# Band attention in a two-layer encoder trunk: edge blocks, and every second pair's middle blocks, copied once as float32 instead of split in two

## Chip, cores, metric

One Trainium2 chip, one of its cores. The metric is the device time of one execution, in microseconds (us). All inputs and the output are float32.

## What is computed

Two layers over 1024 tokens of width 1024. Each layer has three groups of attention heads that read one input projection, and then a SwiGLU feed-forward part:

```python
proj = h @ w_in[l]
qa, ka, va, qb, kb, vb, qc, kc, vc = split_cols(proj, IN_SPLITS)
ya = neighborhood_attention(qa, ka, va, rpb_na[l])            # group A: 4 heads, 8 x 16 neighbours on a 16 x 64 grid
yb = sliding_window_attention(qb, kb, vb, sink_sw[l], t5_table) # group B: 6 heads, |i-j| <= 128, sink logit
yc = axial_attention(qc, kc, vc, gq_ax[l], gk_ax[l])           # group C: 6 heads, dense
y = jnp.concatenate([rms_norm(ya, ga), rms_norm(yb, gb), rms_norm(yc, gc)], axis=-1)
x = x + gt_a * (y @ w_o[l])
```

Inside a head: scores q k^T with a bias, softmax over the keys, then the product of the probabilities with v. Heads are 64 wide.

## The kernel before

**Numbers.** TensorE multiplies float32r operands in one pass each, and float32r keeps fewer bits than float32. Operands are therefore split into a rounded part ("hi") and a rest ("lo"). ScalarE (ACT) makes hi by a converting copy, VectorE (DVE) makes lo by a subtraction (`split_pt`, line 1258). The tile `vs` holds hi and lo of v side by side (64 columns each), so one product with `vs` as the stationary operand gives both parts of v, and `combine` (line 1294) adds the two halves: ACT copies one half out of PSUM, DVE adds the other. A product of probabilities with v thus takes two matmuls, one with the hi and one with the lo of the probabilities.

**Tiles.** Work comes in pairs: 256 queries of one head, as two blocks of 128. A head has four pairs, p = 0 to 3. Group C is dense (`PairC`, 24 pairs in a layer). Groups A and B are banded (`Band`, `PairA`, `PairB`: 16 + 24 = 40 pairs in a layer). For group A the tokens are reordered by columns of the grid, so that its window is a band too. A query block sees its own key block and one to each side. Over a pair there are two *middle* key blocks, seen by all 256 queries, and up to two *edge* blocks: the left one is seen by the first 128 queries only, the right one by the last 128. The pairs p = 0 and p = 3 have one edge block, p = 1 and 2 have two; that makes six in a head and 60 in a layer.

**One band pair**, step by step:

- `qk(c)`, c = 0, 1: two matmuls of 384 columns (256 where the sequence ends), one DVE instruction that adds bias and takes the row maximum (tiles `pr<-sA`, `pr<-sB`), one exponential on ACT with row sums.
- `divide`: a DVE reciprocal of the row sum (`rs<-rs`) and a scaling of the row on POOL (`scale_rows`), once for each c. It is put on the list `unfinished` and taken from there after the next `turn`.
- `turn(0)`: four TensorE transposes of the middle blocks into the PSUM tile `T`, then `split_pt` into two tiles `pt` (ACT then DVE).
- `turn(1)`: one or two transposes of the edge blocks, then `split_pt` into the tile `edge`, which is 256 columns wide for each edge block; the half of the queries that does not see the block is filled with zeros once, in `edges_make`.
- `pv(part)`: matmuls of `vs` with `pt` and `edge` into the PSUM tile `pv`, all 256 columns wide, two for each block. Two pairs share one `pv` tile (512 columns); there is one such tile (`psV`, one buffer), and after the odd pair `combine` empties it.

**Order.** One loop (line 1597) runs over the stream of the 64 pairs of a layer, C then A then B. Step n turns pair n, multiplies pair n-1, and makes the scores of pair n+3, or n+5 in the bands. The last pairs share TensorE with the first rows of the output projection (`ps_o`). In this stage only POOL's order is pinned to the text (line 1595); the orders on TensorE, ACT, DVE and the DMA queue are laid out by the tile framework when the program is built. A statistics step of an earlier group (`ps_st`: float32 sums over partitions by matmul; `isq`: DVE) falls into the stage too.

Every recorded operation has line 49 (the helper `issue`), so the profile is read by tiles.

Of the kernel before, what the change touches and what calls it, by code (L numbers as in the profile page):

```python
# [10 lines left out]
F32 = mybir.dt.float32  # L11
F32R = mybir.dt.float32r
# [7 lines left out]
P = 128  # L20
# [56 lines left out]
def f32(ap):  # L77
    return ap.bitcast(F32)
# [7 lines left out]
def trunk(ctx: ExitStack, tc, A, C, out):  # L86
    nc = tc.nc
    pe, act, dve, pool, sp = (
        Engine(tc, e) for e in (nc.tensor, nc.scalar, nc.vector, nc.gpsimd, nc.sync)
    )  # L90
# [28 lines left out]
    ident = idp.tile([P, P], F32, name="ident")  # L119
# [6 lines left out]
    ident, ones = f32(identr), f32(onesr[:, 0:1])  # L126
# [692 lines left out]
    for l in range(2):  # L819
# [308 lines left out]
        def scale_rows(pr, r):  # L1128
            pool.tensor_scalar(
                out=pr, in0=pr, scalar1=r, scalar2=1.0, op0=ALU.mult, op1=ALU.mult  # L1130
            )
# [14 lines left out]
                pr, s, AF.Exp, bias=rs[:, c : c + 1], accum_out=rs[:, 2 + c : 3 + c]  # L1146
            )

        def divide(pr, rs, c):
            dve.reciprocal(rs[:, 4 + c : 5 + c], rs[:, 2 + c : 3 + c])  # L1150
            scale_rows(pr, rs[:, 4 + c : 5 + c])

        first_pairs = []

        def early_scores():

            p = len(first_pairs)
# [11 lines left out]
            return lambda: [divide(prs[c], rs, c) for c in range(2)]  # L1169

        for oc in range(NE, 8):
            w = wab
# [48 lines left out]
        zB = [bz_tile() for _ in range(2)]  # L1221
        pad(atp, 16)
        gss = {23: gss_tile()}
        edge = []

        def edges_make():
            for _ in range(2):
                e = atp.tile([P, 2, 2, 256], F32R, name="edge", tag="edge", bufs=2)
                for z in range(2):
                    pool.memset(f32(e[:, z, 0, 128:256]), 0.0)  # L1230
                    pool.memset(f32(e[:, z, 1, 0:128]), 0.0)
                edge.append(e)

        edges_used = [0]

        def next_edge():
            edges_used[0] += 1
            return edge[edges_used[0] % 2]

        def edge_ap(e, z, left, right):  # L1240
            flat = e[:, z, :, :].rearrange("p e q -> p (e q)")
            if left and right:
                return flat.rearrange("p (a q) -> p a q", a=4)[:, 0:4:3, :]
            return flat[:, None, 0:128] if left else flat[:, None, 384:512]

        def pt_tile():
            return wp.tile([P, 4, 256], F32R, name="pt", tag="whl", bufs=8)

# [3 lines left out]
        def rs_tile():  # L1252
            return atp.tile([P, 8], F32, name="rs", tag="rs", bufs=6)
# [4 lines left out]
        def split_pt(T, hi, lo):  # L1258
            act.copy(hi, T)
            dve.tensor_tensor(out=lo, in0=T, in1=f32(hi), op=ALU.subtract)  # L1260

        class Pair:
# [5 lines left out]
            def __init__(self, row, vh, p):  # L1268
                self.row, self.vh, self.p = row, vh, p
                self.rs = rs_tile()  # L1270

            def finish(self, c, pr):

                unfinished.append(lambda: divide(pr, self.rs, c))

            def products(self, movs, part):
                if part == 0:
                    if self.p % 2 == 0:
                        open_pv[0] = psV.tile([P, H], F32, name="pv", tag="V")
                    self.pvt = open_pv[0]  # L1280
                cols = slice((self.p % 2) * 256, (self.p % 2) * 256 + 256)
# [45 lines left out]
        unfinished = []  # L1327

        class PairC(Pair):
# [5 lines left out]
            def qk(self, c):  # L1335
                pr = self.pr[c] = pr_tile()
                c_scores(self.h, 2 * self.p + c, c, pr, self.rs)
                self.finish(c, pr)

            def turn(self, c):  # L1340
                if c == 0:
# [9 lines left out]
            def pv(self, part):  # L1351
                self.products(
                    [
                        (kb * 4 + i, self.pt[kb][0][:, i, :], self.pt[kb][1][:, i, :])
                        for kb in range(2)
                        for i in range(4)
                    ],
                    part,
                )
# [38 lines left out]
        class Band(Pair):  # L1398
# [10 lines left out]
            def qk(self, c):  # L1409
                rs, p, sk = self.rs, self.p, self.sk  # L1410
                if c == 0:
                    self.s = psS.tile([P, 2, 512], F32, name=self.name, tag="S")
                s, pr = self.s, self.pr
                j = 2 * p + c
                a, b = self.spans[c]
                for i in range(2):
                    pe.matmul(
                        s[:, c, a:b], self.q[:, j * P : (j + 1) * P],
                        self.k[i][:, (j - 1) * P + a : (j - 1) * P + b],
                        start=(i == 0), stop=(i == 1),  # L1420
                    )
# [12 lines left out]
                self.finish(c, pr[:, c, a:b])  # L1434

            def turn(self, c):
                pr = self.pr
                T = t_tile()
                if c == 0:
                    self.pt = [pt_tile() for _ in range(2)]  # L1440
                    for b in range(2):
                        for i in range(2):
                            pe.transpose(
                                T[:, 2 * b + i, :], pr[:, b, (1 - b + i) * P : (2 - b + i) * P],
                                ident,
                            )
                    hv, lv = (
                        t[:, 0:2, :].rearrange("p i (c q) -> p c i q", c=2) for t in self.pt
                    )
                    split_pt(T.rearrange("p (c i) q -> p c i q", c=2), hv, lv)  # L1450
                    return
                e = self.e = next_edge()
                ne = 0
                if self.left:
                    pe.transpose(T[:, ne, :], pr[:, 0, 0:P], ident)
                    ne += 1
                if self.right:
                    pe.transpose(T[:, ne, :], pr[:, 1, 2 * P : 3 * P], ident)
                    ne += 1
                split_pt(  # L1460
                    T[:, 0:ne, :],
                    edge_ap(e, 0, self.left, self.right),
                    edge_ap(e, 1, self.left, self.right),
                )
# [132 lines left out]
        for n in range(-AHEAD - 1, N + 1):  # L1597
# [22 lines left out]
                    (v_back if n else v_store)(j)  # L1620
            if n == 50:
                yq = qk_tile()
            if n == 8:
                edges_make()
            if n == 54:
                wst = [w_o_stage(k) for k in korder[:2]]
            if n in (55, 59):
# [735 lines left out]
```

## Time and profile before

| | us |
|---|---|
| Median of 3 runs | 2432.55 (2431.05 to 2435.31) |
| The profiled execution, its own time | 2435.83 |
| Its span (first to last instruction) | 2434.1 |
| TensorE (PE) busy | 2362.9 |
| DVE busy | 1785.1 |
| ACT busy | 1203.9 |
| POOL busy | 759.6 |

How to read it: the durations of matmuls overlap, because TensorE is pipelined, and a 256-column matmul is shown with about 0.28 us although the next may start much earlier. A busy PE is therefore not a PE at its peak; what one matmul takes of the engine is read from the distance of the starts in a run of them. "PEld" is the loading of stationary operands beside that. DVE and ACT durations overlap a little too. The stage of the bands lies once in each layer: from the last `combine` of group C to the last of group B, that is 393.2 to 505.8 us in the first layer and 1580.0 to 1692.4 us in the second.

### The profile page before, as it was taken

How to read it: one execution, taken by the hardware profiler on the slowest of the kernel's cores; microseconds unless marked ns; L12 is line 12 of the kernel's file. 1: busy time of each engine (PE TensorE's matmuls, PEld its weight loads, DVE VectorE, ACT ScalarE, POOL GpSimd, SP SyncE). 2: the span in 40 equal slices, each digit the busy share in tenths (PEclk: the TensorE clock that was granted, in tenths of full speed). 3: DMA queues.
4: the chain of work that ended last, by engine and by line, in shares of the span. 5: the costliest groups of instructions: out<-in, count | busy, mean ns of one | idle time of the engine just before them, and what ended most of it. 6: DMA issues, size and time to landing. Idle time of an engine off the chain costs nothing.

```text
span 2434.1 us, 33735 instructions
## 1 busy us (share of the span) xinstructions
PE 2362.9 (97%) x11733; PEld 1963.3 (81%) x11733; DVE 1785.1 (73%) x2950; ACT 1203.9 (49%) x2290; POOL 759.6 (31%) x741
## 2 busy tenths in 40 slices
PE   8999999999999999999999999999999999999998
PEld 5778888788788788788787879987877888888886
DVE  5756899976967788586677589998787545547865
ACT  3421788954543333344543148887454333334443
POOL 1530344620244444300036114464004444430001
PEclk9999999999999999999999999999999999999999
DMA  8478215154245454596434861242534422329643
GB/s 262 151 237 269 61 27 148 43 181 148 87 143 178 156 183 150 166 276 195 144 96 113 277 187 27 58 125 68 191 96 136 142 100 96 103 101 305 206 129 108
DMA packets 305338, 356.98 MB, mean 147 GB/s; under 512 B 51964, under 2 KB 221788, under 8 KB 305168
## 3 DMA queue, kind: packets, MB, share of 16 engines
q1 hardware_dynamic: 283296, 342.07, 44.5%
q10 hardware_dynamic: 21504, 12.59, 2.0%
q8 instruction: 93, 1.52, 0.3%
q14 instruction: 77, 0.63, 0.1%
q0 software_dynamic: 368, 0.17, 0.0%
HBM read 269.79 MB, written 88.63 MB: 147 GB/s over the span
## 4 chain that ended last, share of the span: by engine, by line
PE 50%; DVE 4%; issue 4%; ACT 2%; POOL 1%; DMA 1%; ACTq 0%; SPq 0%; POOLq 0%; DVEq 0%
PE ps_w L49 21%; PE ps_d L49 14%; PE ps_o L49 3%; PE pv L49 2%; PE ps_ab L49 2%; PE ps_v L49 2%; PE T L49 2%; PE sC L49 2%; DMA qkd<-qko 1%; ACT pr L49 1%; PE ps_c L49 1%; POOL ct L49 1%; DVE pt L49 0%; PE ps_st L49 0%; DVE pr L49 0%
## 5 line engine op out<-in xcount | busy, mean ns | idle before, releaser
L49 PE MATMUL ps_d<-wpt 128*128 128x512 f32 x1848 | 424.3, 390 | 2.2 <-ACT wpt L49 1.9
L49 PEld LDWEIGHTS ps_d<-wpt 128*128 128x128 f32 x1848 | 345.6, 188 | 76.2 <-issue 3.0
L49 POOL TENSOR_SCALAR pr<-pr,rs 128x1024 f32<-128x1024 f32 (+2 forms) x248 | 192.8, 780 | 228.8 <-DVE rs L49 203.2
L49 POOL TENSOR_TENSOR sg<-sg,u 128x512 f32<-128x512 f32 x86 | 125.8, 1465 | 356.5 <-ACT sg L49 117.9
L49 PE MATMUL pv<-pt,vs 128*128 128x256 f32 x1088 | 182.5, 296 | 10.8 <-DVE y L49 3.6
L49 ACT CAST wpt<-w 128x512 fp32r<-128x512 f32 x154 | 95.7, 621 | 179.9 <-PE ps_d L49 161.4
L49 DVE TENSOR_TENSOR pt<-T,pt 128x512 fp32r<-128x512 f32 x272 | 178.2, 681 | 6.9 <-ACT pt L49 5.1
L49 PE MATMUL T<-identr,pr 128*128 128x128 f32 x1176 | 172.8, 273 | 1.0 <-DVE pt L49 0.5
L49 ACT CAST pt<-T 128x512 fp32r<-128x512 f32 x272 | 153.0, 586 | 37.8 <-PE T L49 35.8
L49 ACT COPY u<-ps_w 128x512 f32<-128x512 f32 x128 | 75.1, 587 | 193.1 <-PE ps_w L49 192.9
L49 POOL TENSOR_TENSOR wpt<-ws,wpt 128x512 fp32r<-128x512 f32 x80 | 112.3, 1405 | 179.0 <-ACT wpt L49 132.5
L49 DVE TENSOR_TENSOR wpt<-w,wpt 128x512 fp32r<-128x512 f32 x154 | 108.9, 707 | 80.6 <-ACT wpt L49 78.4
L49 PEld LDWEIGHTS pv<-pt,vs 128*128 128x128 f32 x1088 | 145.3, 189 | 27.6 <-DVE y L49 9.8
L49 PEld LDWEIGHTS T<-identr,pr 128*128 128x128 f32 x1176 | 138.2, 140 | 18.3 <-POOL pr L49 1.3
L49 DVE SCALAR_TENSOR_TENSOR acc<-wmt,condT,acc 128x512 f32<-128x512 f32 (+1 forms) x98 | 116.9, 1201 | 44.2 <-DMA wmt<-in_w_mod_dram 43.7
L49 ACT CAST wpt<-ws 128x512 fp32r<-128x512 f32 x176 | 107.7, 622 | 63.4 <-issue 28.2
L49 DVE TENSOR_TENSOR wpt<-ws,wpt 128x512 fp32r<-128x512 f32 x96 | 82.3, 868 | 62.9 <-ACT wpt L49 62.8
L49 DVE TENSOR_TENSOR wpt<-graw,wpt 128x512 fp32r<-128x512 f32 x154 | 109.2, 709 | 19.3 <-ACT wpt L49 19.3
L49 ACT CAST wpt<-graw 128x512 fp32r<-128x512 f32 x154 | 95.0, 617 | 48.2 <-DMA graw<-gpd 40.3
L49 DVE TENSOR_TENSOR ws<-wr 128x512 f32<-128x512 f32 x88 | 80.0, 911 | 49.2 <-POOL wpt L49 46.0
L49 PE MATMUL ps_w<-h22h,wpt 128*128 128x512 f32 x352 | 111.6, 399 | 4.3 <-ACT sg L49 3.6
L49 DVE TENSOR_REDUCE rs<-sC 128x1 f32<-128x1024 f32 x88 | 107.1, 1218 | 7.1 <-PE sC L49 5.2
(299 smaller groups left out, 6024.5 us busy)
## 6 DMA issues: line engine op xcount, KB each, us to landing
wr<-in_w_gu_dram SPq DMA_DIRECT2D x92, 512.0 KB, 4.1
gpd<-sg SPq DMA_DIRECT2D x154, 256.0 KB, 4.4
graw<-gpd SPq DMA_DIRECT2D x76, 512.0 KB, 3.5
w<-in_w_down_dram SPq DMA_DIRECT2D x110, 256.0 KB, 5.4
wmt<-in_w_mod_dram SPq DMA_DIRECT2D x48, 512.0 KB, 6.1
qk<-qkd SPq DMA_DIRECT2D x44, 512.0 KB, 6.7
wst<-in_w_o_dram SPq DMA_DIRECT2D x32, 512.0 KB, 3.9
wmt<-in_w_mod_dram SPq DMA_DIRECT2D x64, 256.0 KB, 3.8
```

Of the source, the lines that this page charges most:

```text
L49: ins = op(*args, **kwargs)
```

## The change

1. Edge blocks (all band pairs): the transposes in `T` are copied once, by DVE, into a float32 tile of one 128-column block each (three buffers), without a hi and lo; no ACT step, no zeros. `pv` multiplies each edge block once, float32 by float32, and only for the 128 queries that see it.
2. Middle blocks of odd pairs (p = 1 and 3): ACT copies `T` once as float32 into one tile `pt`; no subtraction on DVE. `pv` multiplies each of the two blocks once, float32 by float32, 256 columns. Even pairs keep the split in two.
3. All pairs, C too: the two rows' `divide` become one entry in `unfinished`, put there when the second row's scores are done: one reciprocal over two columns, then two scalings on POOL.

```diff
-        def divide(pr, rs, c):
-            dve.reciprocal(rs[:, 4 + c : 5 + c], rs[:, 2 + c : 3 + c])
-            scale_rows(pr, rs[:, 4 + c : 5 + c])
+        def divide(prs, rs):
+            dve.reciprocal(rs[:, 4:6], rs[:, 2:4])
+            for c, pr in enumerate(prs):
+                scale_rows(pr, rs[:, 4 + c : 5 + c])
...
-        def edges_make():
-            for _ in range(2):
-                e = atp.tile([P, 2, 2, 256], F32R, name="edge", tag="edge", bufs=2)
-                for z in range(2):
-                    pool.memset(f32(e[:, z, 0, 128:256]), 0.0)
-                    pool.memset(f32(e[:, z, 1, 0:128]), 0.0)
...
-            def finish(self, c, pr):
-                unfinished.append(lambda: divide(pr, self.rs, c))
+                self.parts = []
+            def finish(self, pr):
+                self.parts.append(pr)
+                if len(self.parts) == 2:
+                    unfinished.append(lambda: divide(self.parts, self.rs))
...
-                for n, (kc, a, b) in enumerate(movs):
+                for n, (kc, at, mvs) in enumerate(movs):
                     if (n < half) != (part == 0):
                         continue
-                    for i, mv in enumerate((a, b)):
+                    for i, mv in enumerate(mvs):
+                        v = vs[:, kc, self.vh, :]
                         pe.matmul(
-                            self.pvt[:, cols], vs[:, kc, self.vh, :], mv,
-                            start=(n == 0 and i == 0), stop=(n == len(movs) - 1 and i == 1),
+                            self.pvt[:, c0 + at.start : c0 + at.stop],
+                            v if mv.dtype == F32R else f32(v), mv,
+                            start=(n == 0 and i == 0),
+                            stop=(n == len(movs) - 1 and i == len(mvs) - 1),
+                            skip_group_check=True,
                         )
...
             def turn(self, c):
                 pr = self.pr
                 T = t_tile()
                 if c == 0:
-                    self.pt = [pt_tile() for _ in range(2)]
+                    whole = self.p % 2
+                    self.pt = [pt_tile() for _ in range(2 - whole)]
+                    if whole:
+                        self.pt = [f32(self.pt[0])]
...
+                    if whole:
+                        act.copy(to[0], T)
+                    else:
+                        split_pt(T, *to)
                     return
-                e = self.e = next_edge()
...
-                split_pt(
-                    T[:, 0:ne, :],
-                    edge_ap(e, 0, self.left, self.right),
-                    edge_ap(e, 1, self.left, self.right),
-                )
+                e = self.e = atp.tile([P, 2, P], F32, name="edge", tag="edge", bufs=3)
...
+                dve.tensor_copy(e[:, 0:n], T[:, 0:n])
 
             def pv(self, part):
                 k0, e = 2 * self.p, self.e
-                movs = [(k0 + i, self.pt[0][:, i, :], self.pt[1][:, i, :]) for i in range(2)]
+                movs = [
+                    (k0 + i, slice(0, 2 * P), [t[:, i, :] for t in self.pt]) for i in range(2)
+                ]
                 if self.left:
-                    movs.append((k0 - 1, e[:, 0, 0, :], e[:, 1, 0, :]))
+                    movs.append((k0 - 1, slice(0, P), [e[:, 0]]))
                 if self.right:
-                    movs.append((k0 + 2, e[:, 0, 1, :], e[:, 1, 1, :]))
+                    movs.append((k0 + 2, slice(P, 2 * P), [e[:, int(self.left)]]))
                 self.products(movs, part)
```

More of the change, by code (lines that the diff above doesn't have):

```diff
@@ L1168, in early_scores @@
             first_pairs.append(prs)
-            return lambda: [divide(prs[c], rs, c) for c in range(2)]
+            return lambda: divide(prs, rs)
         for oc in range(NE, 8):
@@ L1223, in trunk @@
         gss = {23: gss_tile()}
-        edge = []
-        def edges_make():
-            for _ in range(2):
-                e = atp.tile([P, 2, 2, 256], F32R, name="edge", tag="edge", bufs=2)
-                for z in range(2):
-                    pool.memset(f32(e[:, z, 0, 128:256]), 0.0)
-                    pool.memset(f32(e[:, z, 1, 0:128]), 0.0)
[L1232 to L1244, printed above, removed]
         def pt_tile():
@@ L1337, in qk @@
                 c_scores(self.h, 2 * self.p + c, c, pr, self.rs)
-                self.finish(c, pr)
+                self.finish(pr)
             def turn(self, c):
@@ L1353, in pv @@
                     [
-                        (kb * 4 + i, self.pt[kb][0][:, i, :], self.pt[kb][1][:, i, :])
+                        (kb * 4 + i, slice(0, 256), [t[:, i, :] for t in self.pt[kb]])
                         for kb in range(2)
@@ L1433, in qk @@
                 )
-                self.finish(c, pr[:, c, a:b])
+                self.finish(pr[:, c, a:b])
             def turn(self, c):
@@ L1446, in turn @@
                             )
-                    hv, lv = (
-                        t[:, 0:2, :].rearrange("p i (c q) -> p c i q", c=2) for t in self.pt
-                    )
-                    split_pt(T.rearrange("p (c i) q -> p c i q", c=2), hv, lv)
-                    return
-                e = self.e = next_edge()
[L1453 to L1459, printed above, removed]
-                split_pt(
-                    T[:, 0:ne, :],
-                    edge_ap(e, 0, self.left, self.right),
-                    edge_ap(e, 1, self.left, self.right),
-                )
+                    to = [t[:, 0:2, :].rearrange("p i (c q) -> p c i q", c=2) for t in self.pt]
+                    T = T.rearrange("p (c i) q -> p c i q", c=2)
+                    if whole:
+                        act.copy(to[0], T)
+                    else:
+                        split_pt(T, *to)
+                    return
+                e = self.e = atp.tile([P, 2, P], F32, name="edge", tag="edge", bufs=3)
+                n = 0
+                for left, here in ((True, self.left), (False, self.right)):
+                    if here:
+                        src = pr[:, 0, 0:P] if left else pr[:, 1, 2 * P : 3 * P]
+                        pe.transpose(T[:, n, :], src, ident)
+                        n += 1
+                dve.tensor_copy(e[:, 0:n], T[:, 0:n])
             def pv(self, part):
                 k0, e = 2 * self.p, self.e
-                movs = [(k0 + i, self.pt[0][:, i, :], self.pt[1][:, i, :]) for i in range(2)]
+                movs = [
+                    (k0 + i, slice(0, 2 * P), [t[:, i, :] for t in self.pt]) for i in range(2)
+                ]
                 if self.left:
-                    movs.append((k0 - 1, e[:, 0, 0, :], e[:, 1, 0, :]))
+                    movs.append((k0 - 1, slice(0, P), [e[:, 0]]))
                 if self.right:
-                    movs.append((k0 + 2, e[:, 0, 1, :], e[:, 1, 1, :]))
+                    movs.append((k0 + 2, slice(P, 2 * P), [e[:, int(self.left)]]))
                 self.products(movs, part)
@@ L1622, in trunk @@
                 yq = qk_tile()
-            if n == 8:
-                edges_make()
             if n == 54:
```

2 lines of the change are left out of this document (1 added, 1 removed).

## Prediction

> **What bounds the kernel now.** The change touches the band stage, once in each layer, so I read only that stage, and beside it the stage of group C, which runs the same loop. First the view of windows, which gives each engine's busy time in a stretch: the C stage, then the band stage of layer 0 and of layer 1.
>
> ```profile
> core 0: us, PE busy (x) PEld busy (x) DVE busy (x) ACT busy (x) POOL busy (x), PEclk, DMA share, GB/s
> 284.00:375.00 91.00, 90.58 (x650) 82.04 (x648) 85.50 (x138) 78.47 (x143) 40.43 (x43) 1.00 0.07 19
> 393.00:506.00 113.00, 105.41 (x714) 90.52 (x713) 103.21 (x339) 98.91 (x263) 65.31 (x111) 1.00 0.32 94
> 1580.00:1693.00 113.00, 105.63 (x714) 90.55 (x713) 103.43 (x339) 98.67 (x262) 65.39 (x111) 1.00 0.33 95
> ```
>
> The two band stages are alike to 0.3 us, so I work one out and double it. DVE is busy 103 of 113 us and ACT 99. PE's 105 holds overlapping durations, so I count its work. Its groups in the first band stage:
>
> ```profile
> L49 PE MATMUL T<-identr,pr 128*128 128x128 f32 x212 | 35.0, 274 | 0.5 <-DVE pt L49 0.3
> L49 PE MATMUL pv<-pt,vs 128*128 128x256 f32 x160 | 32.2, 302 | 3.5 <-DVE y L49 1.1 <-DVE rs L49 1.1 <-DVE pt L49 0.5
> L49 PE MATMUL pv<-edge,vs 128*128 128x256 f32 x120 | 22.6, 295 | 0.6 <-DVE edge L49 0.6
> L49 PE MATMUL sB<-qk 128*128 128x384 f32 x72 | 20.1, 365 | 0.0
> L49 PE MATMUL sA<-qk 128*128 128x384 f32 x32 | 8.7, 363 | 0.4 <-DVE rs L49 0.4
> L49 PE MATMUL ps_o<-qk,whi 128*128 128x512 f32 x24 | 8.2, 401 | 0.0
> L49 PE MATMUL sB<-qk 128*128 128x256 f32 x24 | 5.9, 326 | 1.3 <-DVE rs L49 1.1
> L49 PE MATMUL ps_o<-qk,wlo 128*128 128x512 f32 x12 | 4.9, 409 | 0.7 <-DVE wlo L49 0.7
> L49 PE MATMUL ps_st<-onesr,gss 128*128 128x1 f32 x32 | 3.7, 245 | 0.0
> L49 PE MATMUL sA<-qk 128*128 128x256 f32 x10 | 2.2, 316 | 0.0
> L49 PE MATMUL ps_r<-identr,rstd 128*128 128x128 f32 x16 | 2.1, 275 | 0.6 <-DVE rs L49 0.6
> ```
>
> What one takes of PE is the distance of starts. In the timeline (start, length of the run, count) it is the length less one instruction's own, over the count less one:
>
> ```profile
> 299.83 1.09 PE L49 MATMUL sC<-qk 128*128 128x512 f32 x4
> 300.75 1.03 PE L49 MATMUL T<-identr,pr 128*128 128x128 f32 x8
> ...
> 403.52 1.84 PE L49 MATMUL ps_st<-onesr,gss 128*128 128x1 f32 x16
> ...
> 423.37 0.64 PE L49 MATMUL pv<-edge,vs 128*128 128x256 f32 x4
> 423.85 0.28 PE L49 MATMUL pv<-pt,vs 128*128 128x256 f32 x1
> ```
>
> So 512 columns take (1.09 - 0.40) / 3 = 0.23 us, a transpose (1.03 - 0.27) / 7 = 0.109, `ps_st` (1.84 - 0.245) / 15 = 0.106, and 256 columns (0.64 - 0.28) / 3 = 0.12; 384 columns, three quarters of 0.23, take 0.175. The counts above times these: transposes 23.1 + 1.7, products 19.2 + 14.4, scores 18.2 + 4.1, `ps_o` 8.3, `ps_st` 3.4: 92.4 us of work. PE is idle 20.6 us of 113, DVE about 10, ACT about 14: no engine is full, three are nearly so. The same count in the C stage, from its three large groups:
>
> ```profile
> L49 PE MATMUL pv<-pt,vs 128*128 128x256 f32 x256 | 38.4, 292 | 0.3 <-DVE y L49 0.2
> L49 PE MATMUL sC<-qk 128*128 128x512 f32 x128 | 35.7, 399 | 0.2 <-ACT pr L49 0.2
> L49 PE MATMUL T<-identr,pr 128*128 128x128 f32 x264 | 35.3, 272 | 0.0
> ```
>
> 30.7 + 29.4 + 28.8 = 88.9 of 91 us: there PE is full, with DVE busy 85.5 beside it. What PE waits for in the band stage, from the view of waits over the same stretch (who waited for whom, total us, times, longest):
>
> ```profile
> PEld sB L49 <- DVE rs L49: 4.2, 13, 0.9
> PEld pv L49 <- DVE pt L49: 3.3, 9, 1.0
> ...
> PEld pv L49 <- DVE y L49: 2.6, 7, 0.7
> ```
>
> The first is a score tile not yet freed by DVE, the second the lo of the middle blocks, the third the one `pv` tile not yet emptied. All three end on DVE. So the band stage is set by DVE, closely followed by ACT, and PE has room.
>
> **The change, part by part** (for one layer: 40 pairs, 20 of them odd, 60 edge blocks).
>
> *PE, float32 products.* The trace has float32 products of 512 columns, with a one-column stationary operand:
>
> ```profile
> 31.95 1.02 PE L49 MATMUL ps_mod<-gm,condT 128*1 128x512 f32 x2
> 32.80 1.02 PE L49 MATMUL ps_mod<-ga,onesr 128*1 128x512 f32 x2
> ```
>
> Each call is two instructions, and the next call starts 0.85 us on. A call of 256 columns costs at least half, 0.425. At most each of its two instructions has also the 0.02 that 512 columns show above a quarter of 0.85 (0.23 against 0.2125), giving 0.465. I take 0.45, since the stationary operand here is 128 wide. An odd pair's two blocks went from 4 x 0.12 = 0.48 to 0.90 (0.85 to 0.93): +0.42, for 20 pairs +8.4 us (7.4 to 9.0). An edge block went from 2 x 0.12 = 0.24 to a call of 128 columns: at least 0.21 (a quarter of 0.85; also two of `ps_st`'s 0.106, which load a 128-wide float32 operand each), at most 0.25. I take 0.23: 60 times -0.01 is -0.6 (-1.8 to +0.6). PE's work rises by 7.8 (5.6 to 9.6), from 92.4 to 100.2.
>
> By the Trainium skill ("TensorE: Matmul & The Clock Gate", Back-to-back issue gap), a 128-column matmul in a stream with its weight loads takes about 81 ns; with the four passes that "FP8 and Floating Point Precision", TensorE Precision Notes, gives a true float32 product, an edge block would be estimated at 0.32 us and the sum below would come out about 11 us higher, at 2434. No row has a 128-column float32 product, and `ps_st`, nearest, points to the lower value.
>
> *DVE.* Its rows in the stage, a float32 copy out of PSUM from the start of the kernel, and a piece of its timeline:
>
> ```profile
> L49 DVE TENSOR_TENSOR pt<-T,pt 128x512 fp32r<-128x512 f32 x39 | 26.6, 682 | 0.7
> L49 DVE RECIPROCAL rs<-rs 128x1 f32<-128x1 f32 x70 | 11.0, 158 | 5.1 <-ACT pr L49 4.4
> ```
>
> ```profile
> L49 DVE COPY xt<-ps_x 128x512 f32<-128x512 f32 x4 | 2.5, 682 | 0.0
> ```
>
> ```profile
> 434.16 0.16 DVE L49 RECIPROCAL rs<-rs 128x1 f32<-128x1 f32 x1
> 434.24 0.28 DVE L49 TENSOR_TENSOR edge<-T,edge 128x128 fp32r<-128x128 f32 x1
> 434.42 0.69 DVE L49 TENSOR_TENSOR pt<-T,pt 128x512 fp32r<-128x512 f32 x1
> 435.02 0.16 DVE L49 RECIPROCAL rs<-rs 128x1 f32<-128x1 f32 x1
> ```
>
> The 20 subtractions of odd pairs go: at a distance of 0.60, -12.0 (-13.6 by duration). A copy out of PSUM takes 682 ns where the subtraction takes 682, so the edge steps stay at their price: 0. Half of the 70 reciprocals go, at 0.08: -2.8. DVE falls from 103.2 to 88.4.
>
> *ACT.* The edge casts go; the odd pairs' copy stays one instruction of 512 columns.
>
> ```profile
> L49 ACT CAST edge<-T 128x256 fp32r<-128x256 f32 x20 | 7.4, 370 | 1.0 <-PE T L49 0.7
> L49 ACT CAST edge<-T 128x128 fp32r<-128x128 f32 x19 | 5.0, 262 | 2.5 <-PE T L49 2.5
> ```
>
> That is -12.4 by duration, some -10.8 at DVE's ratio of distance to duration (0.60 to 0.69). ACT falls from 98.9 to about 88.
>
> *Costed at nothing.* The zeros on POOL go; POOL is busy 65 of 113. The joint reciprocal waits for the second exponential: the first row's scaling starts about half a step later, and POOL's next sink copies and norm work pass ahead of it; its result is due five pairs on (three in C), and a step is 113 / 40 = 2.8 us. On DVE, whatever stands behind that reciprocal (a bias addition or a copy of `T`) waits with it; the row above has 4.4 us of such waits for ACT now, over 70 instructions, so half of them gone bounds it at -2.2, and all of the old wait added once more at +4.4; I take 0. In the C stage DVE's saving lies beside a full PE: 0 (a reciprocal that came late there would show as PE idle above the 2.1 us of now).
>
> *The sum.* After the change PE has 100.2, DVE 88.4, ACT 88. Now the stage runs 113 - 103.2 = 9.8 us above its fullest engine, with three close together; the C stage runs 2.1 above its full PE. Afterwards PE leads by 12, which is like C, but the steps are as short and as chained as now (transpose, copy, product; product, `combine`, next product on the single `pv` tile), so I take a value nearer to today's: 8. The stage then takes 108.2, -4.8 a layer, -9.6 in all. The profiled execution of 2435.83 would take 2426.2; the median of the runs lies 3.3 below that execution, so it goes from 2432.55 to 2423.
>
> **Rivals.**
>
> *PE's idle time stays (slower).* If PE's 20.6 us of idle time are latencies of the chain and not DVE's queue, they stay, and PE's added work is paid in full: +7.8 a layer, +15.6 (11 to 19): 2448. The change is slower by more than 4.9 us in all once less than 5.4 of the 20.6 us go (7.8 - 2.4 a layer). For it: the `pv` tile has one buffer, and its wait (2.6 us) passes through both ACT and DVE. Against it: the two larger rows of the waits view end on DVE instructions that are removed or queue behind removed ones, and the C stage has the same single `pv` tile and hardly any idle PE.
>
> *The gain is eaten (no change).* Idle time falls by PE's added work and no more, to about 13 us: 2432, within 5 us. For it: three engines near 90% trade places, and the order on PE, ACT and DVE is laid out anew when the program is built. Against it: DVE and ACT each lose over 10 us.
>
> *Narrow float32 products cost more.* If the four passes of an edge block were each paced like a `ps_st` instruction, 4 x 0.106 = 0.42, 120 edge blocks cost 0.19 more: +23, so 2446. Against it: 32 `ps_st` instructions serve 16 calls, two each. The skill's 81 ns, above, is the milder form.
>
> *PE full as in C (larger gain).* With 2.1 us above PE's 100.2 the stage takes 102.3: -10.7 a layer, 2411.
>
> **How the numbers follow.** A measurement of this kernel can tell about 0.2%, 4.9 us. Chances: a gain of 5 to 15 us 0.46, more than that 0.11, no change 0.25, idle time stays 0.14, narrow products 0.04. Faster 0.57, same 0.25, slower 0.18. For 8 in 10 the range runs from an excess of 4 us above PE instead of 8 (-8.8 a layer: 2415) to where the idle time falls only to 15 us (100.2 + 15 = 115.2, +2.2 a layer: 2437).
>
> **What would show it.** Right: the window of 113 us shrinks to about 108 in both layers, float32 `pv` calls of 256 columns start 0.45 us apart and edge calls 0.23, DVE busy near 88, and the rows where PE waits for `rs` and `pt` shrink. Wrong: PE idle still above 13 us, waits for `y` or ACT's `cmb` grown, or edge calls above 0.25.

## Result and profile after

The change gains about a tenth of a per cent: ratio 0.9988, 95% interval 0.9979 to 0.9996, which is 2.9 us (1.0 to 5.1) of 2432. The medians of 20 runs each are 2432.32 us before and 2430.68 us after. The forecast was 2423, the range 2415 to 2437. By the bound of 0.2% set in the prediction this is the case "same".

The two profiled executions differ by more, 2435.83 against 2426.46 us, but only part of that is the change. From the last `ps_ab` (the matmuls ahead of C) to the first `ps_w` (the matmuls behind the output projection) the two layers took 336.3 and 335.3 us before and 333.4 and 333.3 after: 4.9 us in all. The other 4.5 us lie where both programs do the same work. The windows of that work (same columns as above: engines' busy time, then the granted clock) of before, then of after:

```profile
589.00:1440.00 851.00, 835.78 (x3700) 686.41 (x3699) 628.17 (x841) 334.36 (x585) 254.74 (x186) 0.99 0.53 168
```

```profile
585.00:1433.00 848.00, 832.67 (x3699) 683.61 (x3698) 628.94 (x839) 332.63 (x584) 256.66 (x185) 1.00 0.53 168
```

The clock is enough for the 3.0 us between them: in the window before, TensorE was granted half its clock (0.50) for four stretches of 3.41 us, in the window after for two, which is 3.4 us of full clock. A single pair of profiles would have shown three times the gain.

The band stage, from the last `combine` of C to the last of B, in the view of windows after:

```profile
core 0: us, PE busy (x) PEld busy (x) DVE busy (x) ACT busy (x) POOL busy (x), PEclk, DMA share, GB/s
393.60:500.20 106.60, 103.18 (x701) 91.94 (x700) 89.42 (x282) 89.55 (x221) 65.66 (x111) 1.00 0.33 99
1575.20:1681.90 106.70, 103.32 (x701) 91.97 (x700) 89.42 (x281) 89.58 (x221) 65.69 (x111) 1.00 0.34 100
```

The stage became 107 us long where it was 113, DVE went from 103.2 to 89.4 and ACT from 98.9 to 89.6. PE's groups in the first layer and, in a second fence, runs of them in the timeline:

```profile
L49 PE MATMUL pv<-pt,vs 128*128 128x256 f32 x160 | 35.6, 342 | 1.0 <-DVE y L49 1.0
L49 PE MATMUL T<-identr,pr 128*128 128x128 f32 x214 | 34.7, 274 | 1.4 <-DVE edge L49 0.5 <-ACT rb L49 0.4 <-ACT pt L49 0.4
L49 PE MATMUL pv<-edge,vs 128*128 128x128 f32 x120 | 19.9, 274 | 0.0
```

```profile
437.34 0.60 PE L49 MATMUL pv<-pt,vs 128*128 128x256 f32 x2
...
495.70 0.61 PE L49 MATMUL pv<-edge,vs 128*128 128x128 f32 x4
...
497.30 1.02 PE L49 MATMUL pv<-pt,vs 128*128 128x256 f32 x4
```

A float32 call is two instructions. Two more instructions of 256 columns make the run 1.02 - 0.60 = 0.42 us longer, so a call takes 0.42; an edge call takes 2 x (0.61 - 0.274) / 3 = 0.22. What PE waits for, from the view of waits:

```profile
PEld pv L49 <- DVE y L49: 3.3, 9, 0.7
...
PEld sB L49 <- DVE rs L49: 2.3, 7, 0.9
```

The wait of `sB` fell from 4.2 to 2.3, that of `pv` for `pt` (3.3) is gone from the list, and the wait for the single `pv` tile, `y`, rose from 2.6 to 3.3.

So the bands gained 6.0 and 5.7 us a layer up to the last `combine`. From there to the first `ps_w`, though, it took 85.1 us instead of 83.3. The first rows of the output projection (`ps_o`) fill gaps of the stage; with fewer gaps, seven of its matmuls fewer fit in (29 in layer 0, below, against 36) and are now done behind it, which is 7 x 0.23 = 1.6 us.

```profile
L49 PE MATMUL ps_o<-qk,whi 128*128 128x512 f32 x19 | 6.6, 410 | 0.0
L49 PE MATMUL ps_o<-qk,wlo 128*128 128x512 f32 x10 | 4.1, 411 | 0.0
```

Up to `ps_w` the bands gained 4.2 and 4.0. And the stage of C, from the last `ps_ab` to its last `combine`, costed at nothing, became 1.3 and 2.0 us longer (140.4 to 141.7, 139.6 to 141.6). Its windows in layer 0, before, then after:

```profile
252.80:393.20 140.40, 137.29 (x980) 124.03 (x979) 129.03 (x232) 119.15 (x226) 61.16 (x66) 1.00 0.19 48
```

```profile
251.90:393.60 141.70, 137.52 (x983) 124.42 (x982) 127.68 (x207) 119.42 (x228) 59.06 (x58) 1.00 0.20 51
```

For both layers together, -8.2 in the bands and +3.3 in C make the -4.9.

### The profile page after: what moved, and what is told of

Its sections match the earlier page's. It is cut to its first block, busy times and chain, and to the rows that moved or that the text cites. A ratio compares the mean times of both kernels' runs of the same rounds, so it can differ in the third digit from the quotient of the medians.

```text
span 2424.7 us, 33399 instructions
## 1 busy us (share of the span) xinstructions
PE 2357.5 (97%) x11733; PEld 1965.5 (81%) x11733; DVE 1758.0 (73%) x2782; ACT 1185.1 (49%) x2210; POOL 759.4 (31%) x725
## 4 chain that ended last, share of the span: by engine, by line
PE 49%; DVE 4%; issue 3%; DMA 3%; ACT 2%; POOL 1%; SPq 0%; ACTq 0%; POOLq 0%; DVEq 0%
PE ps_w L49 21%; PE ps_d L49 14%; PE ps_o L49 4%; PE pv L49 3%; PE T L49 2%; PE ps_v L49 2%; PE sC L49 2%; PE ps_ab L49 1%; DMA qkd<-qko 1%; ACT pr L49 1%; PE ps_c L49 1%; DMA g<-in_gq_ax_dram 1%; POOL ct L49 0%; DMA graw<-gpd 0%; PE sA L49 0%
## 5 line engine op out<-in xcount | busy, mean ns | idle before, releaser
L49 PE MATMUL pv<-pt,vs 128*128 128x256 f32 x1088 | 189.0, 307 | 6.0 <-ACT pt L49 2.7
L49 DVE TENSOR_TENSOR pt<-T,pt 128x512 fp32r<-128x512 f32 x232 | 150.9, 681 | 6.8 <-ACT pt L49 6.0
L49 PEld LDWEIGHTS T<-identr,pr 128*128 128x128 f32 x1176 | 139.9, 140 | 19.6 <-ACT pt L49 1.5
L49 ACT CAST pt<-T 128x512 fp32r<-128x512 f32 x232 | 129.4, 585 | 39.8 <-PE T L49 38.4
L49 ACT CAST wpt<-ws 128x512 fp32r<-128x512 f32 x176 | 107.7, 622 | 62.7 <-issue 28.2
L49 DVE TENSOR_REDUCE rs<-sC 128x1 f32<-128x1024 f32 x88 | 107.2, 1220 | 15.2 <-PE sC L49 10.5
L49 ACT CAST whi<-wst 128x1024 fp32r<-128x1024 f32 x70 | 73.2, 1048 | 86.5 <-PE ps_o L49 52.3
```

Of the source, the lines that this page charges most:

```text
L49: ins = op(*args, **kwargs)
```

## Experiments

Twelve variants, each one profile and several timed runs. The table gives, as the sum of both layers (each figure rounded by itself), how much longer than before the stage of C and the bands up to `ps_w` were in the profile; their sum; and what the timed ratio says. The two agree to within 2.5 us in every row, so what the variants change lies in these two stages. All lengths are taken from one start to another: last `ps_ab`, last `combine` of C, first `ps_w`.

| variant | C, us | bands, us | sum | timed ratio (95%) | in us |
|---|---|---|---|---|---|
| the change | +3.3 | -8.2 | -4.9 | 0.9988 (0.9979 to 0.9996) | -2.9 |
| sep | +3.0 | -4.8 | -1.8 | 0.9983 (0.9973 to 0.9993) | -4.1 |
| joint | 0.0 | -2.8 | -2.8 | 0.9981 (0.997 to 0.9991) | -4.6 |
| edges | +4.9 | -1.5 | +3.4 | 1.001 (0.9997 to 1.0023) | +2.4 |
| all_whole | +5.6 | +9.8 | +15.4 | 1.0059 (1.0044 to 1.0075) | +14.4 |
| lay8 | 0.0 | -6.7 | -6.8 | 0.9974 (0.9963 to 0.9985) | -6.3 |
| lay8_dummy | +0.3 | -3.1 | -2.8 | 0.9982 (0.9971 to 0.9993) | -4.4 |
| lay8_psv2 | +15.2 | -7.2 | +8.0 | 1.0034 (1.0017 to 1.005) | +8.3 |
| lay8_w0 | +0.3 | -10.1 | -9.8 | 0.9959 (0.9944 to 0.9975) | -10.0 |
| w0_two | -0.5 | -3.9 | -4.4 | 0.9977 (0.9966 to 0.9988) | -5.6 |
| w0_act | +0.4 | -11.3 | -10.9 | 0.9958 (0.9944 to 0.9971) | -10.2 |
| w0_pinned | +31.1 | -1.6 | +29.5 | 1.012 (1.0105 to 1.0135) | +29.2 |
| w0_two_pinned | +31.5 | -3.7 | +27.8 | 1.0116 (1.0099 to 1.0133) | +28.2 |

The clock adds a draw of its own to these lengths. In every profiled execution the granted clock falls to 0.50 for five to nine stretches of 3.41 us or longer, most of them outside these stages. Within them, such a stretch lies in one layer's bands of `joint`, `w0_two` (both layer 1), `w0_act` and `w0_pinned` (both layer 0), in one layer's C of `edges` (layer 0) and `all_whole` (layer 1), and in C in both layers of `lay8_psv2`, `w0_pinned` and `w0_two_pinned`. This is the one of `joint` in the view of windows (the 0.50 is the clock):

```profile
1630.30:1633.70 3.40, 3.40 (x16) 3.30 (x16) 0.73 (x6) 1.15 (x3) 1.28 (x3) 0.50 0.00 0
```

Up to the last `combine`, bands with such a stretch were 0.4 to 1.4 us longer than those of the same program's other layer. What brings the stretches on, no run here shows.

**sep: the change with a reciprocal for each row.** The first theory was that the joint reciprocal delays the C stage.

```diff
...
+                c = len(self.parts)
                 self.parts.append(pr)
-                if len(self.parts) == 2:
-                    unfinished.append(lambda: divide(self.parts, self.rs))
+                unfinished.append(lambda: divide_one(pr, self.rs, c))
...
```

> The changed kernel with one reciprocal per row again, as before the change (parts 1 and 2 of the change alone). Theory: the joint reciprocal costs 1.3 and 2.0 us at the entry of the C stage, which was costed at nothing; so from the last ps_ab to the last combine of C this kernel takes 140 us again and not 141.7, from there to the first ps_w of the layer 191.7 as with the change, and in all it runs 7 to 9 us under the kernel before. Rival: the C stage lost its time because the instructions were laid out anew, not because of the reciprocal; then it stays at 141 to 142 and the time at 3 to 5 us under the kernel before.

**joint: the kernel before with the joint reciprocal alone** (part 3 without parts 1 and 2).

> The kernel before with the joint reciprocal alone (part 3 alone). Theory: slower by 3 us, all of it in the C stage (last ps_ab to last combine of C 141 to 142 us in both layers), the band stage as before (195.8 us to the first ps_w, or 1 us less). Rival (new layout, not the reciprocal): C stage as before, 140, and the time within 2 us of the kernel before.

The C stage says no twice. `joint` has the joint reciprocal and no loss in C (139.9 and 140.0 us), `sep` has no joint reciprocal and keeps the loss (142.0 and 141.0). The theory falls. DVE's timeline at the first steps of C shows a new wait (start, length; in brackets the idle time before and what ended it); before:

```profile
257.34 1.29 DVE L49 TENSOR_TENSOR pt<-T,pt 128x512 fp32r<-128x512 f32 x2 [1.93 <-ACT pt L49]
258.54 2.35 DVE L49 TENSOR_REDUCE rs<-sC 128x1 f32<-128x1024 f32 x2
```

after:

```profile
256.40 1.29 DVE L49 TENSOR_TENSOR pt<-T,pt 128x512 fp32r<-128x512 f32 x2 [1.93 <-ACT pt L49]
259.05 2.35 DVE L49 TENSOR_REDUCE rs<-sC 128x1 f32<-128x1024 f32 x2 [1.36 <-DMA qkd<-qko]
```

The row maximum into `rs` uses no data of the store `qkd<-qko`. The new `edge` tiles are smaller (three of 1 KB per partition for two of 4 KB), so what is allocated after them in the same pool moves. The next theory is therefore that an `rs` tile came to lie where the last `qko` tile lay, whose store is still under way; the profile shows no addresses, and `lay8` below tests it. The same wait stands in layer 1 (1.37 us), and in both layers of `sep`, `edges` and `all_whole`, the other variants with three small `edge` buffers and the framework's own order. These four have a C stage of 141.0 us or more. In the framework's order the programs with other buffers have no such wait, and at most 140.4 us (`lay8_psv2`, which takes a tile from C, aside).

**edges: part 1 alone** (`sep` with the middle blocks split in all pairs, `whole = 0`).

> The edge blocks as single float32 copies alone; middle blocks split in two in every pair; one reciprocal per row. DVE's work in the band stage is as before (103 us), ACT loses its 12 us of edge casts, PE's work is about 1 us less. Theory (DVE's queue sets the stage): the stage stays within 2 us a layer of before, that is 194 to 196 us to the first ps_w, and the whole within 4 us. Rival (ACT's queue, or the hop from ACT to DVE, sets it): 4 us a layer go here already, and the whole is 7 to 9 us under the kernel before.

**all_whole: the float32 middle blocks in every pair** (`sep` with `whole = 1`).

> Middle blocks as single float32 copies in every pair, even ones too; edges as in the change; one reciprocal per row. DVE loses 12 us more a layer, PE gains 40 blocks times (0.43 - 0.24), 7.6 us. Theory (with the change PE is already the fullest engine, at 97 of 106.6 us): the stage takes 4 to 7 us a layer more than with the change, 196 to 199 us to the first ps_w, and the whole is within 5 us of the kernel before or slower. Rival (DVE's queue still sets it): 2 to 4 us a layer faster than with the change.

With separate reciprocals the edge blocks give 0.7 and 0.8 us in the two layers' bands (195.1 and 194.9 against 195.9 and 195.7), as the theory for `edges` expected. The odd pairs' middle blocks give another 1.8 and 1.5 (`sep`, 193.4 in both). The even pairs' cost 7.3 a layer (`all_whole`, 200.7 and 200.6, a little more than expected). The window of `all_whole` and one of its waits:

```profile
395.90:510.90 115.00, 111.40 (x699) 96.56 (x697) 82.61 (x297) 90.47 (x221) 63.41 (x111) 1.00 0.31 89
```

```profile
DVE rs L49 <- ACT pr L49: 10.6, 21, 0.8
```

DVE has 82.6 us of work in 115 and waits for the exponentials. PE has 7.2 us more of products than in `sep` (20 pairs whose two blocks take 2 x 0.42 instead of 4 x 0.12). It is the fullest engine by far, and the stage grew by what PE's work grew.

**lay8: the change, with the memory layout of before.** Eight `edge` buffers of 1 KB take the 8 KB of the old two.

```diff
-                e = self.e = atp.tile([P, 2, P], F32, name="edge", tag="edge", bufs=3)
+                e = self.e = atp.tile([P, 2, P], F32, name="edge", tag="edge", bufs=8)
```

> The changed kernel with 8 buffers of the small edge tile instead of 3, so that the pool is as large as before the change (8 KB a partition for edges) and the row-statistics tiles rs lie where they lay. Theory: the entry of the C stage lost its time because the smaller edge tile moved rs onto the last qko tile, whose store is still under way, and the first reduction of the loop waits 1.4 us for that DMA in each layer; here the wait is gone, last ps_ab to last combine of C takes 140 us in both layers again, the stage from there to the first ps_w stays at 191.7, and the whole is 2 to 4 us under the changed kernel, 6 to 9 under the kernel before. Rival: the entry depends on something else in the change; then 141 to 142 as with the change.

The wait is gone, here in DVE's timeline:

```profile
251.72 1.29 DVE L49 TENSOR_TENSOR pt<-T,pt 128x512 fp32r<-128x512 f32 x2 [1.94 <-ACT pt L49]
252.93 2.35 DVE L49 TENSOR_REDUCE rs<-sC 128x1 f32<-128x1024 f32 x2
```

C is back at 139.9 and 140.0. The change and `lay8` have the same instruction lists on ACT and POOL, and on TensorE and DVE lists that differ only in a few places near the end of the bands. So this is the cleanest pair of the study: the loss in C was the layout, and in the timed runs `lay8` lies 3.4 us under the change (-6.3 against -2.9), as expected. The same pair gives the noise of the bands: 191.7 and 191.7 against 191.8 and 193.0, all four without a stretch of half clock, so about 1 us in a layer means nothing.

**lay8_dummy: DVE's work put back.** `lay8`, and DVE does the odd pairs' subtraction into a tile that nobody reads.

```diff
                     if whole:
                         act.copy(to[0], T)
+                        spare_lo = pt_tile()[:, 0:2, :].rearrange("p i (c q) -> p c i q", c=2)
+                        dve.tensor_tensor(out=spare_lo, in0=T, in1=to[0], op=ALU.subtract)
```

> As lay8, with a subtraction of 512 columns put back on DVE in every odd pair, whose result nobody reads; PE's and ACT's work are as in lay8. It gives DVE back the 12 us a layer that the change took from it. Theory (DVE's queue set the stage, and its relief is the gain): the stage to the first ps_w grows from 191.7 to 196 to 200 us a layer, since PE keeps its added work; 4 to 8 us a layer slower than lay8. Rival (the gain came from the shorter chain, transpose, one copy, product, and DVE had room): within 1.5 us a layer of lay8.

```profile
396.20:506.30 110.10, 105.63 (x705) 93.02 (x704) 99.91 (x301) 89.58 (x221) 64.13 (x111) 1.00 0.33 94
```

DVE has 10.3 us more (89.6 to 99.9). The bands take 3.3 and 2.0 us more up to the last `combine`, 2.5 and 1.1 up to `ps_w`. The result lies between the theory (4 to 8) and the rival (less than 1.5): with PE's added products in place, a third or less of DVE's added work shows in the time. That is no proof against DVE as the limit of the kernel before. PE has about 97 us of work here, so only the last 2.9 of DVE's 99.9 stand above it.

**lay8_psv2: a second `pv` tile**, taken from the tiles `T` (`PS_T = 2` for 3).

> As lay8, with two pv tiles in PSUM and two T tiles instead of one and three. Theory (what PE still idles, 9 to 10 of 106.7 us, is mostly the wait for the one pv tile to be emptied, 4.3 us in the waits, and the refilling after it): 2 to 4 us a layer faster in the bands. Rival (the third T tile is worth more): slower by 2 us a layer or more, in the C stage too.

In the bands the wait for `y` is gone, but they take 192.3 and 192.0, as without it. So the theory fails: the growing wait for `y` in the profile after was not what held the bands. The price in C, which the rival expected, is there: 147.5 and 147.7, 7.6 us more. Up to 3.4 us of that can be the clock, which was 0.50 for 6.83 us in each layer's C. The third `T` is missed without that too: in 80 us of C at clock 1.00, 556 matmuls ran here and 576 in `lay8`.

**lay8_w0: parts 1 and 3 without part 2** (`lay8` with `whole = 0`: edge blocks in float32, joint reciprocal, middle blocks split in all pairs).

> As lay8, but the middle blocks of odd pairs are split in two as before: what is left of the change is the edges and the joint reciprocal. The band stage had 195.8 before, 193.7 and 195.0 with the joint reciprocal alone, 195.0 with the edges alone. If these two add, 193 to 194; then the middle blocks of odd pairs are worth about 2 us a layer (191.7), 4 us in all. Rival (the edges and the reciprocal are the whole gain): 191.5 to 192.5, and the same time as lay8.

```profile
391.60:499.00 107.40, 102.64 (x709) 88.54 (x707) 99.36 (x302) 89.04 (x221) 64.43 (x111) 1.00 0.33 97
```

190.7 and 190.8 us to `ps_w`, 1.1 and 2.2 *less* than with part 2, and less than either expectation. So part 2 gained 1.8 and 1.5 with separate reciprocals and nothing, or a little less than nothing, with the joint one. The comparison with `lay8_dummy` points to what took the gain: DVE (99.9 and 99.4) and ACT (89.6 and 89.0) are equally busy in both, PE has 7.2 us of products more in `lay8_dummy`, and `lay8_dummy` takes 3.6 and 3.4 us longer up to `ps_w`. The products that part 2 adds on PE cost at least what its relief of DVE brings (2.5 and 1.1, `lay8_dummy` against `lay8`); the order differs between these programs too. Timed, the two are not told apart for certain (0.9959 and 0.9974, with intervals that overlap). `lay8_w0` is the fastest version of the study beside `w0_act`: 2422.39 us, and its interval lies below that of the change, which also bears the loss in C.

**w0_two: is it the number of reciprocals or their place?** `lay8_w0` with one reciprocal for each row, both at the place of the joint one.

```diff
-            dve.reciprocal(rs[:, 4:6], rs[:, 2:4])
             for c, pr in enumerate(prs):
+                dve.reciprocal(rs[:, 4 + c : 5 + c], rs[:, 2 + c : 3 + c])
                 scale_rows(pr, rs[:, 4 + c : 5 + c])
```

> As lay8_w0 (edges and joint division, middle blocks split in every pair), but the joint division has two reciprocals of one column each instead of one of two columns; both still stand after the second row's exponential. It tells why one reciprocal per pair helps. Theory (place: a reciprocal behind the first row's exponential made DVE's queue stand still, 5.1 us a layer of waits for ACT before, 2.0 in lay8_w0; at the later place it does not): the stage stays within 1 us a layer of lay8_w0's 190.8. Rival (count: 35 instructions fewer, at 0.08 us): 2 to 3 us a layer slower, 193 to 194.

Up to `ps_w` it takes 193.3 and 194.3, 2.7 and 3.5 more than `lay8_w0` (layer 1 with a stretch of half clock), by 35 instructions of 0.16 us. The groups of reciprocals in the bands of `edges`, `w0_two` and `lay8_w0`, in this order:

```profile
L49 DVE RECIPROCAL rs<-rs 128x1 f32<-128x1 f32 x70 | 11.0, 159 | 5.6 <-ACT pr L49 5.0
```

```profile
L49 DVE RECIPROCAL rs<-rs 128x1 f32<-128x1 f32 x70 | 10.9, 158 | 2.4 <-ACT pr L49 1.8
```

```profile
L49 DVE RECIPROCAL rs<-rs 128x2 f32<-128x2 f32 x35 | 5.7, 161 | 2.1 <-ACT pr L49 1.7
```

The later place halves the waits (5.6 to 2.4), as the lower bound in the prediction had it (`edges` also has three edge buffers and not eight); the number of instructions leaves them as they are. By the pair `w0_two` and `lay8_w0` the number counts, as the rival said. But the instruction lists of these two programs differ along the whole of both stages, on TensorE, DVE and ACT: the framework laid the orders out anew. The last two variants ask how much of it is that.

**w0_act: the edge copies on ACT** (`lay8_w0` with `act.copy` for `dve.tensor_copy`).

> As lay8_w0, but the edge blocks are copied by ACT instead of DVE. In lay8_w0's band stage DVE is idle 7.6 us of 107.4 and ACT 18.3. Theory (DVE's queue still sets the stage): DVE loses 10 to 13 us of copies, ACT is then as full as it was before the change, and the stage takes 1 to 3 us a layer less, 188 to 190, the whole 11 to 15 us under the kernel before. Rival (ACT's casts of T then stand behind exponentials, as before the change): 191 to 193, no gain over lay8_w0 or a loss.

190.6 (with a stretch of half clock) and 189.7, between theory and rival: up to `ps_w` the same as `lay8_w0` within the noise, though 10.4 us went from DVE (99.4 to 89.0) and 6.6 to ACT (89.0 to 95.6). Up to the last `combine` the layer without the stretch is 2.3 us shorter (107.5 to 105.3). There the fullest engine is now ACT, 3.8 us below DVE's 99.4.

**w0_pinned and w0_two_pinned: the same two kernels in another order.** ACT's order is pinned to the text, as POOL's is, in `lay8_w0` and in `w0_two`.

```diff
-        pin((pool,), True)
+        pin((pool, act), True)
...
-        pin((pool,), False)
+        pin((pool, act), False)
```

> lay8_w0 with the same work, but with ACT's order pinned to the order of the text as POOL's is; so the orders on ACT, DVE and TensorE all come out different. It sizes what a new order alone does. Theory 'the parts cost what their instructions cost': from the last combine of C to the first ps_w stays within 1 us of lay8_w0's 190.7/190.8 in both layers. Rival 'a good part of the differences of 1 to 3 us between the variants is the order laid out anew': it moves by 2 us or more, either way.

> w0_two (a reciprocal of one column for each row, at the later place) with ACT's order pinned in the same way: the pair with w0_pinned repeats the comparison of lay8_w0 and w0_two in another order. Theory 'the 35 reciprocals taken away are themselves worth 2.6 to 3.5 us a layer': it is 2 to 4 us a layer longer than w0_pinned from the last combine of C to the first ps_w. Rival 'that gain was the order that the framework happened to lay out': less than 1 us longer, or shorter.

Both rivals came true. The same work in another order (`w0_pinned` against `lay8_w0`) costs 15.6 and 15.2 us in C and 4.5 and 3.9 in the bands. The clock is the smaller part of it: the stretches of half clock can make up 3.4 and 1.7 us of these figures in C, and the bands of layer 1, 3.9, hold none. At the start of C the first row maximum comes earlier in this order and waits 1.31 us for a store `qkd<-qko`, in spite of the eight buffers, and ACT's first exponential waits for such a store for 5.08 us (layer 0); so the padding of `lay8` removes the wait in the framework's order only. The window of the bands and the largest wait of ACT in `w0_pinned`:

```profile
407.30:519.50 112.20, 104.27 (x703) 88.56 (x703) 97.94 (x299) 89.97 (x222) 64.17 (x110) 0.98 0.32 90
```

```profile
ACT pr L49 <- DVE rs L49: 12.3, 14, 2.0
```

With the same instructions ACT waits 12.3 us for row maxima instead of 2.8. And in this order two reciprocals are not slower: 193.9 and 194.0 against 195.2 (with a stretch of half clock) and 194.7, no difference beyond the noise. So the price of 2.7 to 3.5 us for 35 reciprocals is no property of the reciprocals alone; it belongs to them together with the order that is laid out around them. In the framework's own order the joint reciprocal was ahead in all four pairs (before and `joint`, `sep` and the change, `edges` and `lay8_w0`, `w0_two` and `lay8_w0`), by 1.7 to 4.5 us in the layers without a stretch of half clock (`edges` and `lay8_w0` differ in the number of edge buffers too). How much of that is the instructions and how much the order stays open; no run here holds DVE's order fixed.

## Why the prediction was off

**Right: the prices on PE.** 0.42 us for a float32 call of 256 columns (0.45 predicted) and 0.22 for an edge call (0.23). By the counts, transposes 214 x 0.109, products 80 x 0.12, 80 x 0.21 and 120 x 0.112, scores 22, `ps_o` 29 x 0.23, the small ones 5: about 97 us of PE work, where 100.2 was predicted; the `ps_o` matmuls that left are half of that difference. The rival of narrow products is refuted: an edge call takes 0.22 us and not 0.42, because it is two instructions, each 0.112 after the last, and not four. The milder estimate of 0.32 was worked out from about 81 ns for a 128-column matmul, which the Trainium skill states ("TensorE: Matmul & The Clock Gate", Back-to-back issue gap). It was too high too: an instruction takes longer here, 0.112 us, but there are only two of them.

**Right: DVE and ACT.** 89.4 and 89.6 us against 88.4 and 88. The edge step on DVE kept its price, as costed (256 columns; before, then after):

```profile
L49 DVE TENSOR_TENSOR edge<-T,edge 128x256 fp32r<-128x256 f32 x20 | 8.2, 411 | 0.0
```

```profile
L49 DVE COPY edge<-T 128x256 f32<-128x256 f32 x20 | 8.3, 414 | 0.7 <-PE T L49 0.7
```

**Right, with a gap: the stage.** -4.8 a layer was predicted; up to the last `combine` it was -6.0 and -5.7, with PE idle for some 10 us (8 predicted, above 13 would have refuted it). PE's work came out 3 us smaller than costed and the idle time 2 us larger, two errors of opposite sign. The rule behind the sum, a stage some 8 to 10 us longer than its fullest engine, fits every variant in the framework's own order. In layers without a stretch of half clock the excess up to the last `combine` is 8 to 10 us where DVE is fullest (`edges`, `joint`, `lay8_w0`, `w0_two`, `lay8_dummy`) or ACT (`w0_act`), and about 10 to 12 where PE is (the others). But the prediction's stage ended at that `combine`, where work that had filled PE's gaps is only pushed out: up to `ps_w` -4.2 and -4.0 are left.

**Wrong: the C stage at nothing.** The step looked for a late reciprocal and bounded that. `joint` shows that it costs nothing in C. The loss of 1.3 and 2.0 us a layer came from the size of the `edge` tile, most likely by way of the address of another tile (no run shows addresses), and `lay8` gives it back. In sum, the two layers gained 11.6 us up to the last `combine` (9.6 predicted); 3.5 of them came back in the output projection and 3.3 were lost in C.

**Half right: what bounds the bands, and which part pays.** The prediction said that DVE sets the stage before the change and that PE leads after it, and it did not divide the gain among the parts. Of the 14.8 us that DVE was to lose, 12.0 were part 2's, and yet part 2 gains 1.8 and 1.5 us without the joint reciprocal and loses 1.1 and 2.2 with it, the latter barely above the noise. By the rule of the fullest engine this is little surprise: parts 1 and 3 take DVE, and with it the top, from 103.0 us to 99.4, and part 2 then takes the top only to 97, because its own products make PE the fullest. The rule is not the whole account, though. `lay8_dummy` is longer than `lay8_w0` with the same work on DVE, and `w0_pinned` lies 14 us above its fullest engine with the same instructions, so the chain between the engines, in the order laid out for it, counts too. Nor do the parts add up: alone, the edge blocks give 0.7 and 0.8 and the joint reciprocal 2.2 and 0.7 (the 0.7 with a stretch of half clock); together 5.2 and 4.9 (`lay8_w0`).

That DVE set the stage before the change is likely, not shown. `edges` takes 8.3 us of work from ACT and none from DVE there, and the stage gains 0.7 and 0.8 us up to the last `combine`; `joint` takes 2.1 us from DVE, and the stage gains 2.2 (layer 0, without a stretch of half clock), but `joint` moves the reciprocal as well.

**The rivals.** "PE's idle time stays" fell: 20.6 us became 10. "The gain is eaten" has its time nearly right (2432) and its mechanism not: the idle time fell below the 13 us that it gives, and more than half of the gain was lost outside the stage. "PE full as in C" was not reached. That the measured 2430.68 lies in the range is thus partly luck: a gain in the stage that was larger than forecast made up for some of two losses that were not in the sum.

## What to carry to other kernels

With several engines near 90% busy, work taken off the fullest one counts only until the next one is fullest, and what the change adds to that next one has to be paid. To see what the time saved on one engine is worth, put the same amount back as a dummy, and end the stage where the next one starts, not at the last instruction that you changed. If the orders are laid out when the program is built, every edit is also a new order; a few us between variants are then a draw, until a variant with the same work in another order says how large the draw is. After a change to a tile's size, look at the first waits of the stages that share its pool for a releaser that has nothing to do with the data; padding the tile back to its old size tells at once. And before you compare a stage between two profiles, read its granted clock: the layers of one program, one with and one without a short stretch of half clock, differed by up to 1.4 us here.

## What the hardware showed beyond that

A float32 product with a 128-wide stationary operand is two instructions, each 0.21 us after the last at 256 columns and 0.112 at 128, so at 128 columns it costs no more than two float32r passes of 256 columns (2 x 0.12). Executions of one program spread over 10 us or more (before 2427.32 to 2438.49, after 2423.02 to 2435.74 in 20 runs each), about four times the gain measured here. In the two profiled ones the granted clock was 0.991 and 0.994. It falls to 0.50 in separate stretches, of 3.41 us at the shortest, nine in the execution before and six in the one after. In the 20 runs of the change the mean clock went with the time, from 0.990 (2430.54 us and more) to 0.995 (2423.02).
